# A two-block transformer forward pass: one queue for the first inputs, norm factors applied later, wider MLP entries, and the RWKV chunk matrices kept as 64x64 blocks

## The chip, the cores and the metric

The kernel runs on one core of a Trainium2 chip. The metric is the device time of one execution in microseconds; the time before is the median of three runs. A profiled execution, taken by the hardware profiler, gives the trace. TensorE is called PE here, its weight load PEld, VectorE DVE, ScalarE ACT, GpSimd POOL and SyncE SP.

## The reference

The input x has 256 tokens of 1024 features, in float32. Two blocks follow one another. The part that the change rewrites most is the RWKV7 recurrence of the first block:

```python
def rwkv7_scan(r, w, k, v, a_vec, b_vec):
    """S_t = S_{t-1} diag(w_t) + (S_{t-1} a_t) b_t^T + v_t k_t^T ; y_t = S_t r_t. All (B,T,H,N)."""
    def step(s, inp):
        r_t, w_t, k_t, v_t, a_t, b_t = inp
        sa = jnp.einsum('bhvk,bhk->bhv', s, a_t)
        s = s * w_t[:, :, None, :] + sa[..., None] * b_t[:, :, None, :] + v_t[..., None] * k_t[:, :, None, :]
        return s, jnp.einsum('bhvk,bhk->bhv', s, r_t)

def first_block(x, ...):
    h = rms_norm(x, mix_norm_g)
    x = x + hybrid_mixer(h, ...)   # h @ w_in; short conv, stick-breaking attention, RWKV7, spatial gating,
                                   # four sigmoid gates over their projections, @ w_o
    h = rms_norm(x, ffn_norm_g)
    x = x + conv_glu_ffn(h, w_up, ffn_conv_w, w_down)
    return rms_norm(x, final_norm_g)

def second_block(x, mem, ...):     # layer 0: pool mixer, layer 1: sliding-window attention with sinks
    for l in range(2):
        proj = rmsnorm(h, norm_mix[l]) @ w_in[l]
        main, mq = proj[..., :768], proj[..., 768:]
        main_out = pool_mixer(main, ...) if l == 0 else swa_sink_attention(...)
        mem_out = memory_attention(...)
        h = h + jnp.concatenate([main_out, mem_out], axis=-1) @ w_out[l]
        h = h + sq_relu_mlp(rmsnorm(h, norm_mlp[l]), w_up[l], w_down[l])
    return h
```

The recurrence has 4 heads of 64 channels. The pool mixer takes, in 4 groups of 192 channels, the mean over the last 2, 4, 8 or 16 tokens less the token itself, and multiplies each group by a 192x192 matrix.

## The kernel before

**Products.** Every weight is loaded from HBM by `load_split` (L193): SP issues the transfer to a buffer `raw`, ACT casts it to fp32r (`wh`), DVE subtracts (`wl` = raw − wh). There are four buffers of each. A product is then three fp32r matmuls into one PSUM group (`mm3`, L207): high by high, high by low, low by high. I call these the main matmuls. The small products of the mixers are plain fp32, and in the trace an fp32 product is two instructions.

**Order.** PE's order is the order in which the program issues its products. The main line of the program issues groups of main matmuls and calls `tick()` (L234) after each. `tick()` lets every generator that was put `beside` the main line go on by its rate (0.5 steps a tick unless given, 0.6 for RWKV, L897); a generator issues one step of small work and yields. `finish()` runs generators to their end at once. The work within `urgent()` gets a higher priority on DVE and ACT.

**The start.** Seven cold matmuls on a zeroed buffer run while the inputs come. ACT issues the five transfers of xT (L464), SP those of the weights; `split_scaled` makes the pair `xp` of x times the norm's gain, and `fm_part` multiplies it by blocks 9 and 7 of `w_in`, piece by piece of xT (`z_first`). The norm's factor per token is not applied to x but later to the products: a generator (`input_norm`) sums the squares, POOL raises the mean to the power −0.5 (`rtok`, L379), and PE spreads it over the partitions. For the RWKV columns this is used in `shifted`, which `finish()` (after block 6) precedes.

**RWKV.** `rwkv()` (L556) works on 4 chunks of 64 tokens, two chunks to a half `b` of 128 tokens. For each half and head it makes the products of `bt` and `ktl` with `ar` (64 channels deep), masks them to the two chunks on the diagonal (`at`, 128x128 for each head), inverts the triangular matrix by doubling in five levels (`LEVELS`), and then goes over the chunks one by one: `rc`, `uc`, the state `st`, and the output `yt`. In the inversion X, Y and PX are 128x128 for each head with zeros off the two 64x64 blocks. A level makes one product X,at, one Y,PX and (but for the last) a transposition of Y, for four heads and both halves. The masked products, in the words of the code:

```python
at = [mt([P, 2, 4, P], "at", bufs=4) for _ in range(2)]
...
def level(b, lhs, rhs, w):
    o = psum("A")
    for h in range(4):
        TE.matmul(o[:, 64 * h : 64 * h + 64], lhs[:, h], half(rhs[:, h], w), start=True, stop=True)
    return packed(o)
```

**MLP entry.** Each MLP multiplies by `w_up` in blocks of 256 features (`fm_blocks`, L271), each by halves of the 1024 input features. The first 512 input features are ready before the others: after the first half of the first block's product, `finish(first_half)` issues the transpositions and pairs (`features`) that make the rest.

**Pool layer.** `main_block` makes the main columns by blocks, `pool_tile` the windowed means of 128 channels (a product with `bands`, then `dd` on DVE and the pair `dp`), `pool_product` the 192x192 products of a group, which end in the pair `y`. `out_half` multiplies four of the eight blocks of `y` by `w_out2` and adds the sum; it runs twice, first for blocks 4 to 7 and after `pool_product(0)` for 0 to 3. Memory attention (`att`, two generators) runs beside.

## Time and profile before

| | |
|---|---|
| median of 3 runs | 1030.14 us (1028.31 to 1031.03) |
| profiled execution, its own time | 1030.78 us |
| its span | 1028.9 us, 16258 instructions |
| PE busy | 1009.8 us (98% of the span), 6216 matmul instructions |
| DVE busy | 699.2 us (68%) |
| ACT busy | 558.2 us (54%) |
| POOL busy | 142.7 us (14%) |
| DMA | 176.39 MB, mean 171 GB/s |

The span goes from the first instruction to the last; 1.9 us of the profiled execution lie around it. Busy is the share of the span in which an engine has an instruction under way. A PE row gives the time from the first start to the last end of a run of equal instructions, and matmuls are pipelined, so that what a matmul costs is the distance from its start to the next one's, and not its length. A wait in square brackets is the idle time of the engine just before the row, with what ended it.

### The profile page before, as it was taken

How to read it: one execution, taken by the hardware profiler on the slowest of the kernel's cores; microseconds unless marked ns; L12 is line 12 of the kernel's file. 1: busy time of each engine (PE TensorE's matmuls, PEld its weight loads, DVE VectorE, ACT ScalarE, POOL GpSimd, SP SyncE). 2: the span in 40 equal slices, each digit the busy share in tenths (PEclk: the TensorE clock that was granted, in tenths of full speed). 3: DMA queues.
4: the chain of work that ended last, by engine and by line, in shares of the span. 5: the costliest groups of instructions: out<-in, count | busy, mean ns of one | idle time of the engine just before them, and what ended most of it. 6: DMA issues, size and time to landing. Idle time of an engine off the chain costs nothing.

```text
span 1028.9 us, 16258 instructions
## 1 busy us (share of the span) xinstructions
PE 1009.8 (98%) x6216; PEld 876.8 (85%) x6216; DVE 699.2 (68%) x1101; ACT 558.2 (54%) x966; POOL 142.7 (14%) x137
## 2 busy tenths in 40 slices
PE   8999999999999999999999999999999999999998
PEld 7889987778899999988888888888898668888886
DVE  4787467687747888865576777746467877776452
ACT  5653556454557655545664655535365556555432
POOL 0110001121000000001210244400011103443000
PEclk9999999999999999999999999999999999999999
DMA  8535353356555555565534455555553325555661
GB/s 288 181 122 162 111 179 110 127 176 243 174 184 205 190 184 183 184 189 186 179 120 154 161 195 188 184 189 187 199 210 122 103 90 172 185 188 186 191 217 63
DMA packets 50590, 176.39 MB, mean 171 GB/s; under 512 B 5776, under 2 KB 6928, under 8 KB 50128
## 3 DMA queue, kind: packets, MB, share of 16 engines
q1 hardware_dynamic: 49392, 173.51, 51.0%
q10 hardware_dynamic: 1008, 1.57, 0.4%
q8 instruction: 49, 0.80, 0.3%
q0 software_dynamic: 112, 0.27, 0.1%
q14 instruction: 29, 0.24, 0.1%
HBM read 174.28 MB, written 1.05 MB: 170 GB/s over the span
## 4 chain that ended last, share of the span: by engine, by line
PE 88%; DVE 7%; ACT 2%; issue 1%; POOL 1%; DMA 1%; ACTq 0%; DVEq 0%; POOLq 0%
PE mm L126 76%; PE ps L126 11%; DVE wl L203 3%; ACT wh L202 1%; DMA a<-in_xT 0%; DMA raw<-in_w_in 0%; DVE a L343 0%; POOL a L1131 0%; DVE a L349 0%; DVE sc L346 0%; DVE mxs L1175 0%; ACT sc L1193 0%; DVE yt L349 0%; DVE sq L349 0%; POOL r L379 0%
## 5 line engine op out<-in xcount | busy, mean ns | idle before, releaser
L203 DVE TENSOR_TENSOR wl<-raw,wh 128x1024 fp32r<-128x1024 f32 (+2 forms) x318 | 387.3, 1219 | 237.9 <-ACT wh L202 236.0
L202 ACT CAST wh<-raw 128x1024 fp32r<-128x1024 f32 (+2 forms) x318 | 328.4, 1034 | 348.9 <-PE mm L126 315.9
L126 PE MATMUL mm<-a,wh 128*128 128x256 f32 (+1 forms) x1536 | 370.1, 323 | 2.9 <-DVE a L343 2.2
L126 PE MATMUL mm<-a,wl 128*128 128x256 f32 x1024 | 288.5, 282 | 0.0
L126 PEld LDWEIGHTS mm<-a,wh 128*128 128x128 f32 x1536 | 256.2, 190 | 30.3 <-DVE a L343 4.3
L126 PEld LDWEIGHTS mm<-a,wl 128*128 128x128 f32 x1024 | 194.8, 190 | 0.2 <-issue 0.2
L126 PE MATMUL mm<-wh,u 128*128 128x512 f32 x512 | 158.6, 389 | 0.0
L126 PE MATMUL mm<-wh,a 128*128 128x512 f32 (+1 forms) x512 | 145.8, 358 | 0.0
L126 PEld LDWEIGHTS mm<-wh,u 128*128 128x128 f32 x512 | 96.1, 188 | 20.0
L1249 POOL TENSOR_TENSOR u<-gate,u 128x256 fp32r<-128x256 f32 x64 | 84.5, 1322 | 170.2 <-ACT u L1248 119.8
L126 PEld LDWEIGHTS mm<-wh,a 128*128 128x128 f32 x512 | 91.0, 189 | 14.1 <-issue 1.2
L126 PE MATMUL mm<-wl,u 128*128 128x512 f32 x256 | 99.6, 389 | 0.0
L126 PE MATMUL mm<-wl,a 128*128 128x512 f32 (+1 forms) x256 | 90.0, 352 | 0.0
L126 PEld LDWEIGHTS mm<-wl,u 128*128 128x128 f32 x256 | 48.1, 188 | 9.8
L126 PE MATMUL mm<-wh,ff 128*128 128x512 f32 x176 | 54.9, 390 | 0.0
L126 PEld LDWEIGHTS mm<-wl,a 128*128 128x128 f32 x256 | 48.5, 190 | 5.5
L126 PE MATMUL mm<-wh,y 128*128 128x512 f32 x128 | 43.2, 406 | 0.9 <-ACT y L338 0.5
L346 DVE SCALAR_TENSOR_TENSOR cv<-mm,pv,cv 128x255 f32<-128x255 f32 x88 | 42.2, 479 | 1.7 <-ACT cv L1093 0.2
L126 PEld LDWEIGHTS mm<-wh,ff 128*128 128x128 f32 x176 | 33.0, 188 | 6.9
L126 PE MATMUL mm<-wl,ff 128*128 128x512 f32 x88 | 34.3, 389 | 0.0
L346 DVE SCALAR_TENSOR_TENSOR gate<-gate 128x256 f32<-128x256 f32 x64 | 31.9, 501 | 2.0
L349 DVE TENSOR_TENSOR gate<-mm,gate 128x256 f32<-128x256 f32 (+1 forms) x68 | 29.5, 434 | 3.7 <-ACT gate L1245 2.9
(342 smaller groups left out, 1188.1 us busy)
## 6 DMA issues: line engine op xcount, KB each, us to landing
raw<-in_w_up SPq DMA_DIRECT2D x108, 512.0 KB, 4.4
raw<-in_w_dn SPq DMA_DIRECT2D x86, 512.0 KB, 4.3
raw<-in_w_in SPq DMA_DIRECT2D x36, 512.0 KB, 3.8
raw<-in_w_gate SPq DMA_DIRECT2D x32, 512.0 KB, 3.7
raw<-in_w_out SPq DMA_DIRECT2D x16, 512.0 KB, 3.8
raw<-in_outs SPq DMA_DIRECT2D x8, 512.0 KB, 3.6
raw<-in_w_mkv SPq DMA_DIRECT2D x8, 512.0 KB, 3.6
raw<-in_w_o SPq DMA_DIRECT2D x8, 512.0 KB, 4.4
```

The source lines that it names most:

```text
L126: ins = f(*a, **k)
L202: S.copy(wh[:, :m], raw[:, :m])
L203: V.tensor_tensor(out=wl[:, :m], in0=raw[:, :m], in1=wh[:, :m].bitcast(F32), op=ALU.subtract)
L346: return V.scalar_tensor_tensor(out=o, in0=a, scalar=sc, in1=b, op0=op0, op1=op1)
L349: return V.tensor_tensor(out=o, in0=a, in1=b, op=op)
L1249: G.tensor_tensor(out=u.l[:, n], in0=sq, in1=u.h[:, n].bitcast(F32), op=ALU.subtract)
```

## The change

- xT's transfers are issued by SP, each piece ahead of the weights that it is multiplied with; the constants `cm`, `ci` and `cb`, which SP issued between the weights, come later.
- Blocks 6 and 8 of `w_in` are both multiplied before `finish()`; then the factor is applied to all four blocks.
- The RWKV matrices are kept as two blocks of 64x64, one below the other (`[P, 4, 64]` in place of `[P, 4, 128]`). `chunks` multiplies each chunk's block on its own 64 rows and its own 64 columns of the array: rows 0 to 63 with columns 0 to 63 of the output, rows 64 to 127 with 64 to 127, into one PSUM buffer. The transposition of Y is a product with a 64x64 identity. The products with `ar` are issued by chunk and by head of a pair, the two heads of a pair into different buffers. `rc` and `uc` are no longer zeroed.
- Two more yields stand ahead of the transposition of `yt`, the rate of `rwkv` is 0.65, memory attention has one yield more, `features` is urgent.
- `fm_blocks` begins with the first halves of two blocks (four PSUM buffers) ahead of `finish(first_half)`.
- In the pool layer `out_half` is no longer used there: `pool_product(0)` comes directly behind the last `pool_tile`, and each half of the output columns is one product over all eight blocks of `y`, in the order 4, 2, 0, 6, with `finish(*atts)` ahead of 6.

The diff, cut to its core:

```diff
@@ -285,11 +285,19 @@
-        for i, src in enumerate(srcs):
+        os_ = [psum_mm(), psum_mm(), psum_mm(), psum("M")]
+        for a in (0, 4):
+            if a:
+                finish(first_half)
+            for i in range(2):
+                w = load_split(srcs[i][:, a : a + 4], 4)
+                for j in range(2):
+                    part(os_[2 * i + j], w, j, a, a + 4)
+                    if a:
+                        yield os_[2 * i + j]
+        for src in srcs[2:]:
...
             for a in (0, 4):
-                if a and not i:
-                    finish(first_half)
@@ -330,8 +338,9 @@
                 TE.transpose(o[:, i * P : i * P + P], h[:, j, k * P : k * P + P], ident)
-            for k in (k0, k0 + 1):
-                use(k, o[:, (k - k0) * T : (k - k0) * T + T])
+            with urgent():
+                for k in (k0, k0 + 1):
+                    use(k, o[:, (k - k0) * T : (k - k0) * T + T])
@@ -458,11 +467,6 @@
-    FIRST = ((0, 1), (1, 2), (2, 4), (4, 6), (6, 8))
-    xT = t8()
-    for a, b in FIRST:
-        nc.scalar.dma_start(out=xT[:, a:b], in_=I["xT"][:, a:b])
@@ -490,15 +494,16 @@
-    xp = pair8()
+    xT, xp = t8(), pair8()
     z_first = {b: psum("M") for b in (3, 1)}
-    for a, b in FIRST:
+    for a, b in ((0, 1), (1, 2), (2, 4), (4, 6), (6, 8)):
+        nc.sync.dma_start(out=xT[:, a:b], in_=I["xT"][:, a:b])
...
     CB = load_const(cp, "cb")
-    ident, bones, ones = CB("ident"), CB("bones"), CB("ones")
+    ident, bones, ones, ident2 = CB("ident"), CB("bones"), CB("ones"), CB("ident2")
@@ -533,17 +538,14 @@
-    for b in (0, 2):
-        o = fm_block(I["w_in"][6 + b], xp)
-        if b == 0:
-            finish()
-            for z in (3, 1):
-                shifted(z, z_first[z])
-            wlo = q2("wlo", "A")
-            nc.sync.dma_start(out=wlo, in_=I["lora"])
-            CM = load_const(m1, "cm")
-            CI = load_const(m1, "ci")
+    z_first.update((b, fm_block(I["w_in"][6 + b], xp)) for b in (0, 2))
+    finish()
+    for b, o in z_first.items():
         shifted(b, o)
+    wlo = q2("wlo", "A")
+    nc.sync.dma_start(out=wlo, in_=I["lora"])
+    CM = load_const(m1, "cm")
+    CI = load_const(m1, "ci")
@@ -628,24 +630,40 @@
+        chunk = [slice(0, CH), slice(CH, P)]
+        def chunks(o, n, lhs, rhs):
+            for h in range(4):
+                for c in chunk:
+                    TE.matmul(o[c, n * h : n * h + n], lhs(h, c), rhs(h, c), start=True, stop=True)
+            return o[:, : 4 * n]
...
         for b in range(2):
-            bs = slice(b * P, b * P + P)
-            at = [mt([P, 2, 4, P], "at", bufs=4) for _ in range(2)]
-            for h in range(4):
-                j, hs = h // 2, slice(64 * (h % 2), 64 * (h % 2) + 64)
-                o = psum("A")
+            at = [mt([P, 2, 4, CH], "at", bufs=4) for _ in range(2)]
+            o = [psum("A") for _ in range(2)]
+            for j in range(2):
                 for i, src in enumerate((bt, ktl)):
-                    TE.matmul(o[:, 256 * i : 256 * i + 256], src[hs, j, bs], ar[hs, :, j, bs], start=True, stop=True)
-                o4 = o.rearrange("p (i a t) -> p i a t", i=2, a=2)
+                    for c in chunk:
+                        tk = slice(b * P + c.start, b * P + c.stop)
+                        for e in range(2):
+                            at_ = (2 * j + i) * P
+                            TE.matmul(o[e][c, at_ : at_ + P], src[chunk[e], j, tk], ar[chunk[e], :, j, tk],
+                                      start=True, stop=True)
+            for e in range(2):
+                o4 = o[e].rearrange("p (j i a t) -> p a i j t", j=2, i=2, a=2)
                 for a in range(2):
-                    tt(at[a][:, :, h], o4[:, :, a], over(CM("mar")[:, a * P : a * P + P], 2))
+                    tt(at[a][:, :, e::2], o4[:, a], CM("mar")[:, a * CH : a * CH + CH].rearrange(
+                        "p (i j t) -> p i j t", i=1, j=1).to_broadcast([P, 2, 2, CH]))
...
-            X, Y, PX = (q2(n, "A", shape=(P, 4, P)) for n in ("X", "Y", "PX"))
+            X, Y, PX = (q2(n, "A", shape=(P, 4, CH)) for n in ("X", "Y", "PX"))
             G.memset(PX, 0.0)
-            S.copy(X, over(ident, 4))
-            S.copy(Y, over(ident, 4))
+            S.copy(X, over(ident2, 4))
+            S.copy(Y, over(ident2, 4))
@@ -653,13 +671,11 @@
         for b in range(2):
-            o = psum("A")
-            for h in range(4):
-                TE.transpose(o[:, h * P : h * P + P], atA[b][:, 0, h], ident)
+            o = chunks(psum("A"), CH, lambda h, c: atA[b][c, 0, h], lambda h, c: ident2[c])
...
         for m in LEVELS:
-            nb = P // (2 * m)
+            nb = CH // (2 * m)
@@ -668,30 +684,24 @@
             def packed(o):
-                return o[:, :256].rearrange("p (h n m) -> p h n m", h=4, m=m)
+                return o.rearrange("p (h n m) -> p h n m", h=4, m=m)
...
-            def level(b, lhs, rhs, w):
-                o = psum("A")
-                for h in range(4):
-                    TE.matmul(o[:, 64 * h : 64 * h + 64], lhs[:, h], half(rhs[:, h], w), start=True, stop=True)
-                return packed(o)
+            def level(lhs, rhs, w):
+                return packed(chunks(psum("A"), CH // 2, lambda h, c: lhs[c, h], lambda h, c: half(rhs[c, h], w)))
...
             for b in range(2):
-                S.copy(half4(Pm[b], 0), level(b, atA[b][:, 0], Xm[b], 0))
+                S.copy(half4(Pm[b], 0), level(atA[b][:, 0], Xm[b], 0))
...
             for b in range(2):
-                V.copy_predicated(half4(Ym[b], 1), lmask(f"my{m}"), level(b, Pm[b], Ym[b], 1))
+                V.copy_predicated(half4(Ym[b], 1), lmask(f"my{m}"), level(Pm[b], Ym[b], 1))
...
                 for b in range(2):
-                    o = psum("A")
-                    for h in range(4):
-                        TE.transpose(o[:, h * P : h * P + P], Ym[b][:, h], ident)
-                    S.copy(flat(Xm[b]), o)
+                    S.copy(flat(Xm[b]), chunks(psum("A"), CH, lambda h, c: Ym[b][c, h], lambda h, c: ident2[c]))
@@ -708,23 +718,22 @@
             rc, uc = scr([P, 256], "rc", "A"), scr([P, 256], "uc", "A")
-            G.memset(rc, 0.0)
-            G.memset(uc, 0.0)
...
             o = psum("A")
-            for h in range(4):
-                vs = slice(64 * h, 64 * h + 64)
-                TE.matmul(o[cs, vs], atA[b][:, 1, h, cs], vtk[:, b, vs], start=True, stop=(c == 0))
-                if c:
-                    TE.matmul(o[cs, vs], ar[:, 0, h // 2, tk], st[:, h], start=False, stop=True)
+            vss = [slice(64 * h, 64 * h + 64) for h in range(4)]
+            last = lambda h: h == 3
+            for h, vs in enumerate(vss):
+                TE.matmul(o[cs, vs], atA[b][cs, 1, h], vtk[cs, b, vs], start=(h == 0), stop=(c == 0 and last(h)))
+            if c:
+                for h, vs in enumerate(vss):
+                    TE.matmul(o[cs, vs], ar[:, 0, h // 2, tk], st[:, h], start=False, stop=last(h))
...
             o = psum("A")
-            for h in range(4):
-                vs = slice(64 * h, 64 * h + 64)
-                TE.matmul(o[cs, vs], Ym[b][:, h, cs], rc[:, vs], start=True, stop=True)
+            for h, vs in enumerate(vss):
+                TE.matmul(o[cs, vs], Ym[b][cs, h], rc[cs, vs], start=True, stop=True)
@@ -749,12 +758,13 @@
             o = psum("A")
-            for h in range(4):
-                vs = slice(64 * h, 64 * h + 64)
-                TE.matmul(o[cs, vs], atR[b][:, 1, h, cs], vtk[:, b, vs], start=True, stop=False)
-                if c:
-                    TE.matmul(o[cs, vs], ar[:, 1, h // 2, tk], st[:, h], start=False, stop=False)
-                TE.matmul(o[cs, vs], atR[b][:, 0, h, cs], uc[:, vs], start=False, stop=True)
+            for h, vs in enumerate(vss):
+                TE.matmul(o[cs, vs], atR[b][cs, 1, h], vtk[cs, b, vs], start=(h == 0), stop=False)
+            for h, vs in enumerate(vss):
+                TE.matmul(o[cs, vs], atR[b][cs, 0, h], uc[cs, vs], start=False, stop=(c == 0 and last(h)))
+            if c:
+                for h, vs in enumerate(vss):
+                    TE.matmul(o[cs, vs], ar[:, 1, h // 2, tk], st[:, h], start=False, stop=last(h))
@@ -790,6 +800,8 @@
         tt(yt, yt, sq, ALU.add)
+        yield
+        yield
@@ -894,7 +906,7 @@
-    rw = beside(rwkv(), 0, 0.6)
+    rw = beside(rwkv(), 0, 0.65)
@@ -1204,6 +1216,8 @@
                 ts(sc[:, a, at(tb)], sc[:, a, at(tb)], rc[:, i : i + 1])
+        if swa is None:
+            yield
@@ -1358,19 +1372,32 @@
-    beside(tiles((5, 4, 3, 2)))
+    tl = beside(tiles((5, 4, 3, 2)))
...
     main_block(0)
+    finish(tl)
...
     pool_tile(0)
-    finish()
     h1 = tok8()
-    out_half(0, 4, y, residual, h1)
...
     g, sums, done = to_mlp(0)
-    tf = out_half(0, 0, y, lambda j, c: h1[:, j, c], h1, done)
+    for cb in range(2):
+        o = [psum_mm() for _ in range(2)]
+        for a in (4, 2, 0, 6):
+            if a == 6:
+                finish(*atts)
+            w = load_split(I["w_out2"][0, cb, :, a : a + 2], 2, 512)
+            for j in range(2):
+                for k in (a, a + 1):
+                    mm3(o[j], y[:, k, j * P : j * P + P], w[:, k - a], k == 4, k == 7)
+                tick()
+        c = slice(512 * cb, 512 * cb + 512)
+        for j in range(2):
+            with urgent():
+                tt(h1[:, j, c], o[j], residual(j, c), ALU.add)
+        tf = done(h1, cb)
```

How the order moves, on SP and PE.

SP's queue at the start, before (`raw` is a weight, `a` here is xT, `cb`, `cm`, `ci` are constants):

```order
L459 DMA pv<-in_pv 128x248
L200 DMA raw_99<-in_w_in 128x256
L200 DMA raw_111<-in_w_in 128x256
L200 DMA raw_125<-in_w_in 128x256
L200 DMA raw_137<-in_w_in 128x256
L447 DMA cb_269<-in_cb 128x384
```

and after:

```order
L468 DMA pv<-in_pv 128x248
L500 DMA a_3_88<-in_xT 128x256
L201 DMA raw_95<-in_w_in 128x256
L201 DMA raw_107<-in_w_in 128x256
L500 DMA a_3_88<-in_xT 128x256
L201 DMA raw_122<-in_w_in 128x256
```

The first piece of xT now stands second in SP's queue and the second piece fifth, where ACT issued them before.

PE in one level of the inversion, before: a transposition of Y for both halves between main matmuls.

```order
L126 MATMUL mm_1078<-a_4_94,wl_1123 128x256
L126 MATMUL ps_1139<-cb_269,Y_875 128x128 x4
L126 MATMUL ps_1145<-cb_269,Y_933 128x128 x4
L126 MATMUL mm_1078<-a_4_94,wh_1122 128x256 x2
L126 MATMUL mm_1078<-a_4_94,wl_1123 128x256
```

and after, the same place:

```order
L127 MATMUL mm_1118<-a_4_89,wl_1121 128x256
L127 MATMUL ps_1137<-cb_269,Y_865 64x64 x8
L127 MATMUL ps_1147<-cb_269,Y_907 64x64 x8
L127 MATMUL mm_1118<-a_4_89,wh_1120 128x256 x2
L127 MATMUL mm_1118<-a_4_89,wl_1121 128x256
```

Four transpositions of 128x128 have become eight products of 64x64; the steps X,at and Y,PX change in the same way, from 128x64 x4 to 64x32 x8.

PE at the end of the pool layer, before (`bands` belongs to the last `pool_tile`, `y` to the product with `w_out2`, `dp` to `pool_product(0)`):

```order
L126 MATMUL mm_5745<-bands,uh 128x256
L126 MATMUL mm_5745<-bands,ul 128x256
L126 MATMUL mm_5755<-wh_5758,y_5239 128x512
L126 MATMUL mm_5755<-wl_5759,y_5239 128x512
L126 MATMUL mm_5755<-wh_5758,y_5239 128x512 x2
```

and after:

```order
L127 MATMUL mm_5847<-bands,uh 128x256
L127 MATMUL mm_5847<-bands,ul 128x256
L127 MATMUL mm_5863<-dp_5358,wh_5858 128x256
L127 MATMUL mm_5872<-dp_5358,wh_5858 128x256
L127 MATMUL mm_5884<-dp_5358,wh_5858 128x256
L127 MATMUL mm_5884<-dp_5359,wh_5858 128x256
```

Behind the last bands 48 matmuls with `y` stood before the first with `dp`; now the first with `dp` stands there.

## Rows read from the trace of the kernel before

**Rows 1.** the page: the chain that ended last, share of the span by engine

```profile
PE 88%; DVE 7%; ACT 2%; issue 1%; POOL 1%; DMA 1%; ACTq 0%; DVEq 0%; POOLq 0%
```

**Rows 2.** PE's waits by releaser: us in total, times, longest us

```profile
PE ps L126 <- ACT a L342: 3.0, 1, 3.0
PE ps L126 <- POOL rtok L379: 2.2, 1, 2.2
PE mm L126 <- DVE a L343: 2.2, 4, 1.1
PE ps L126 <- DVE yt L349: 2.1, 1, 2.1
...
PE ps L126 <- DVE sc L353: 0.8, 2, 0.7
PE ps L126 <- DVE uc L728: 0.7, 1, 0.7
...
PE mm L126 <- DVE y L343: 0.3, 1, 0.3
```

**Rows 3.** windows: length, busy us (x) of PE, PEld, DVE, ACT, POOL; PEclk, DMA

```profile
10.40:14.30 3.90, 3.82 (x17) 3.60 (x18) 2.52 (x7) 2.66 (x7) 0.00 (x0) 0.56 1.03 388
14.30:20.00 5.70, 5.70 (x50) 5.70 (x49) 4.69 (x9) 3.70 (x8) 0.00 (x0) 1.00 0.76 247
66.00:78.00 12.00, 11.24 (x71) 8.68 (x70) 11.23 (x27) 6.71 (x9) 0.53 (x1) 1.00 0.26 89
```

**Rows 4.** timeline of the start: start, us, engine, instruction, [idle before]

```profile
0.74 5.21 ACTq L464 DMA_DIRECT2D a<-in_xT  x5
...
1.19 6.33 PE L126 MATMUL mm<-cold 128*128 128x256 f32 x14 [1.19 <-DVE cold L476]
...
10.48 1.10 PE L126 MATMUL ps<-a,wh 128*128 128x256 f32 x3 [2.95 <-ACT a L342]
...
23.79 0.40 PE L126 MATMUL mm<-a,wh 128*128 128x256 f32 x2
```

**Rows 5.** timeline of PE around a step X,at and around sgw,vg

```profile
84.55 1.90 PE L126 MATMUL ps<-X,at 128*128 128x64 f32 x16
...
86.26 0.48 PE L126 MATMUL mm<-a,wh 128*128 128x256 f32 x2
...
86.94 0.28 PE L126 MATMUL mm<-a,wl 128*128 128x256 f32 x1
...
87.14 0.66 PE L126 MATMUL ps<-sgw,vg 128*64 128x128 f32 x8
...
87.73 0.50 PE L126 MATMUL mm<-a,wh 128*128 128x256 f32 x2
```

**Rows 6.** groups by form: names, shapes, xcount | busy us, mean ns

```profile
L126 PE MATMUL ps<-cb,Y 128*128 128x128 f32 x32 | 4.1, 272 | 0.0
```

**Rows 7.** timeline of PE in a state update

```profile
154.90 0.22 PE L126 MATMUL ps<-vtk,ktm 64*64 64x64 f32 x1
154.90 0.27 PE L126 MATMUL ps<-uc,btm 64*64 64x64 f32 x2
154.96 0.22 PE L126 MATMUL ps<-vtk,ktm 64*64 64x64 f32 x1
```

**Rows 8.** windows, ar alone, sum of 3 stretches

```profile
sum 6.59, PE 6.22 PEld 4.11 DVE 0.00; mean PE 2.07 PEld 1.37 DVE 0.00
```

**Rows 9.** timeline of PE, products with ar

```profile
69.04 0.38 PE L126 MATMUL ps<-ar,ktl 64*128 64x256 f32 x1
69.25 0.38 PE L126 MATMUL ps<-ar,bt 64*128 64x256 f32 x1
69.25 0.38 PE L126 MATMUL ps<-ar,ktl 64*128 64x256 f32 x1
```

**Rows 10.** timeline at the end of the pool layer

```profile
541.39 0.28 PE L126 MATMUL mm<-bands,ul 128*128 128x256 f32 x1
...
542.82 0.86 ACT L338 CAST dp<-dd 128x256 fp32r<-128x256 f32 x2 [2.15 <-DVE dd L349]
```

19 lines of the change are left out of this document (9 added, 10 removed).

## The prediction

> **What bounds the kernel now.** I read the page first: the chain of work that ended last lies 88% on PE [rows 1]. So the time is the sum of PE's instructions and of the few places where PE waits, and an edit counts only if it shortens one of the two. PE's own waits, grouped by releaser, are the second view: there is one long wait for each of ACT a (3.0), POOL rtok (2.2) and DVE yt (2.1), and a few shorter ones [rows 2]; those shown are 11.3 us of a span of 1028.9. Third come the windows of the start: after its first idle stretch PE gets a granted clock of 0.56 from 10.4 to 14.3 and does 17 matmuls there, where the next 5.7 us hold 50 at clock 1.00 [rows 3]. Last, the timelines, for what a small product costs and what it costs to go to it and come back.
>
> The sum is made against the profiled execution, 1030.78 us. The median of the runs shown is 0.64 lower, within their spread, so I don't correct for it. I take 0.3%, about 3.1 us, as the least difference that a measurement of this kernel can tell from none.
>
> **1. The start.** ACT issues the five xT transfers for 5.21 us and only then loads its tables, and the first real matmul stands at 10.48, after 2.95 us of idle; the cold matmuls, which begin at 1.19, are done at 7.52 (1.19 + 6.33) [rows 4]. The phase of 96 matmuls of 120 ns (17 in 3.90 us at the low clock, 50 in 5.70 at the full one [rows 3]) would be 11.5 us long; it takes 13.3, from 10.48 to the next phase at 23.79 [rows 4]. After, SP issues the first piece of xT directly after pv, ahead of the weights, and ACT has no issues and one table load fewer in front of its first casts. If the first casts end before 7.5, PE goes on without a gap: 10.48 − 7.5 = 3.0, and 13.3 − 11.5 = 1.8 if the clock then stays at 1.00, since PE was busy and granted 1.00 up to there. Five more issues stand ahead of the later weights on SP's queue, and cb, cm and ci, which stood ahead, go behind; I take off 0.5 for one late piece. Bounds: 0 (the low clock stays and the data are no earlier) and −5.3 (no late piece, and the last cold matmul followed at once). **−4.3.**
>
> **2. Norm factors.** rtok's spread over the partitions stands 4 real matmuls behind its sum before and 12 after, so 8 more of 120 ns cover the wait of 2.2 [rows 2]: **−1.0**, between 0 and −2.2.
>
> **3. RWKV matrices.** One product of the levels is now eight 64x64 tiles on the diagonal (rows and columns 0–63, then 64–127) in place of four full ones. In the trace an fp32 product is two instructions. Before: one step X,at is 16 instructions from 84.55 to 86.26, 1.71 us or 107 ns each, and leaves one following matmul 0.1 late [rows 5]. Ten steps (80 instructions X,at, as many Y,PX) make 17.1. The transposes cb,Y are 32 instructions in four trips, 4.1 us busy [rows 6]; a fifth trip (cb,at) makes 5.1, and some 0.2 of each lies over the next matmul: 4.1. Together 21.2. After: 160 + 160 + 128 + 32 = 480 instructions. What a 64x64 product costs shows in the state updates: their starts come two at a time, 0.06 us from pair to pair [rows 7], so 29 ns each: 13.9. These pairs share the rows and differ in columns; pairs on the diagonal of the array are not in the trace, and that is this sum's open point (rivals). Going to a narrow tile and back costs more than to a full one: before sgw,vg the last matmul takes 0.20 (86.94 to 87.14) in place of 0.12, the eight products take 0.59 where four pairs at X,at's 0.11 would be 0.44, and the two matmuls behind take 0.50 [rows 5] where two take 0.40 [rows 4], some 0.35 in all; two matmuls behind X,at take 0.48, a trip of 0.09. So 0.26 for each of 15 trips (10 steps, 4 + 1 transposes): +3.9. Sum: 13.9 + 3.9 − 21.2 = **−3.4**. That the evictions on ACT and DVE are half as wide helps, since DVE is busy 11.23 of 12.0 us from 66 to 78 [rows 3], but PE is fed by main matmuls there, so I count nothing.
>
> The products with ar: 32 instructions in three stretches, 6.59 us [rows 8]. After, 64 of half the columns, in four quadrants. Where bt and ktl run in pairs, a pair follows the one before it by 0.21 [rows 9]. After, in pairs and at half the columns, 32 × 0.105 = 3.4; and there are half the evictions to wait for, 0.3. 6.6 + 0.3 − 3.4 = **−3.5**, between −2.5 (waits stay) and −5 (four at once).
>
> The chunk steps keep their number of products, but change tile shape three times more: **+0.4**. Three main matmuls now stand between rc's product and the state's in every chunk; the wait for uc, 0.7 in one chunk [rows 2], can come up in the others: **+0.5**, between −0.7 and +1.8.
>
> **4. yt.** Two steps more before the transposes, at a higher rate. As many main matmuls as before (36) stand between the bonus product and the transposes, but on DVE one foreign operation lies between the bonus's copy and yt's last addition where four lay. If the three are 0.7 long on average, the wait of 2.1 [rows 2] goes, with 0.1 of restart: **−2.2**, at least −1.
>
> **5. Entries of the two MLPs.** Their first halves are now 32 matmuls in front of finish(first_half), 5.6 us, where 16 (2.8 us) stood. The wait for DVE a (2.2 in four places, 1.1 the longest [rows 2]) ends; with the restarts of the weight load that the waits view leaves out, 2.6: **−2.6**, at least −1.5. What comes next is the same work of ACT and DVE with twice the cover.
>
> **6. Pool layer.** A further step in memory attention takes away the wait for sc, 0.8 [rows 2]. In return the product of group 0 now stands right behind the last bands, where 48 matmuls with y stood. Its input is not ready: the last band starts at 541.39, and the cast to dp, behind dd on DVE, ends at 543.68 (542.82 + 0.86) [rows 10]. PE, ready at 541.51, waits some 2.1. The wait for DVE y ahead of the last w_out2 products, 0.3 [rows 2], goes, with its restart 0.5. −0.8 + 2.1 − 0.5 = **+0.8**, at most +2.5. The four DVE additions that are gone lie beside PE, at nothing; where features are now urgent the order of DVE and ACT is that of before, at nothing too.
>
> **Sum:** −4.3 − 1.0 − 3.4 − 3.5 + 0.4 + 0.5 − 2.2 − 2.6 + 0.8 = −15.3, so 1030.8 − 15.3 = 1015.5, taken as **1015**. With the bounds above, its own range is 1008 to 1022.
>
> **Rivals.** *The diagonal pairs take turns.* Both tiles of a pair write the same PSUM bank, in other partitions. In the trace products on different rows (bt and ktl with ar, both at 69.25 [rows 9]) run in pairs, but write different banks; the pairs that share a bank [rows 7] differ in columns alone. Neither is the new case. If they take turns, the 480 products cost 58 ns each: 27.8 + 3.9 − 21.2 = +10.5 in place of −3.4, and the kernel takes 1015.5 + 13.9 = **1029**. For it: all pairs on different rows avoid a common bank in this code. Against: a tile pair on the diagonal shares neither rows, columns nor partitions, and both nearest rows show pairs. The Trainium skill, TensorEngine Tiling (Array Packing), section Restrictions and Gotchas, says that different row tiles cannot access the same PSUM bank at one time, which speaks against this edit: by it the pairs take turns. No row of this trace shows it either way.
>
> *The weight load isn't covered (slower).* If a small product cannot load its weights while the one before it still runs in another tile, it costs what X,at costs, 107 ns [rows 5], for a quarter of the work: 480 × 0.107 + 3.9 − 21.2 = +34, with the −11.9 of the rest +22, **1053**. It decides from 61 ns on (480 × 0.061 + 3.9 − 21.2 = 12.0, the gain of all the rest), and shows as slower from 67. Against it: the state updates, at 29 ns each [rows 7], can't have an uncovered load.
>
> *New waits.* The tighter distances (products behind the bands, steps at a rate of 0.65, uc in three chunks) together cost 6 more than counted, or the start gains nothing: **1020**. For it: DVE is near full from 66 to 78 [rows 3]. Against: away from the places counted PE has hardly waited at the old distances, and most have grown.
>
> **How the numbers follow.** Forecast 0.70; turns 0.18; new waits 0.07; load not covered 0.05. The predicted time is the forecast's, 1015. The range reaches from its low end, 1008, to the rival of the turns, 1029, and leaves out the slower rival and some of both tails. Faster by over 0.3% is below 1027.1: forecast, new waits and a small part of the turns, 0.79; within 0.3%, 0.15 (turns, beside better luck elsewhere); slower 0.06.
>
> **What would show it.** In the changed trace the first real matmul should stand near 7.5 with granted clock 1.00 up to 20; the wait for ACT a in the start should be gone. Sixteen instructions of a level's step should take some 0.5 us for one half of the sequence, the 480 together some 14 to 18; about 28 us says turns, 50 the uncovered load. The waits for yt and for DVE a in front of the MLPs should be gone, rtok's about 1.2, and a new one of about 2 should stand behind the last bands, for ACT or DVE dp. The ar products should take about 3.4 us. The forecast is wrong if PE's start-to-start time of a 64x64 product on the diagonal is 50 ns or more, or if waits of PE above 1 us stand in new places.

## The result, and the profile after

| | before | changed |
|---|---|---|
| median | 1029.22 us (1026.40 to 1031.03, 4 runs) | 1016.11 us (1015.11 to 1016.87, 4 runs) |
| profiled execution | 1030.78 us, span 1028.9 | 1015.11 us, span 1013.3 |
| ratio | | 0.9874, 95% interval 0.9848 to 0.9901 |

The kernel is some 13 us faster; 1015 was forecast. In the experiment with full-size matrices one of eight executions took 1223.95 us at a granted clock of 0.75; the time given there is the median of the other seven. The page of the changed kernel, busy times and the chain that ended last:

```profile
PE 999.4 (99%) x6528; PEld 866.8 (86%) x6528; DVE 690.0 (68%) x1089; ACT 553.9 (55%) x965; POOL 143.4 (14%) x129
...
PE 89%; DVE 5%; DMA 2%; ACT 2%; issue 1%; POOL 1%; SPq 0%; DVEq 0%; ACTq 0%; POOLq 0%
```

PE is 10.4 us less busy, though it executes 312 instructions more (6528 for 6216), and the chain lies on PE as it did [rows 1]. The rest of the 15.6 us between the two spans is waits.

PE's waits by releaser, in the same columns as [rows 2]:

```profile
PE mm L127 <- ACT dp L347: 1.4, 1, 1.4
PE ps L127 <- ACT wh L203: 1.3, 1, 1.3
...
PE mm L127 <- DVE ul L355: 0.9, 1, 0.9
PE ps L127 <- POOL rtok L388: 0.8, 1, 0.8
PE mm L127 <- DVE dp L348: 0.7, 2, 0.4
PE mm L127 <- DVE gate L355: 0.7, 1, 0.7
PE ps L127 <- DVE ktl L358: 0.6, 1, 0.6
...
PE mm L127 <- DVE a L358: 0.2, 1, 0.2
...
PE mm L127 <- DVE a L352: 0.2, 1, 0.2
```

The waits for ACT a (3.0), DVE yt (2.1), DVE sc (0.8) and DVE uc (0.7) of [rows 2] are gone, those for DVE a have shrunk from 2.2 to 0.2 and 0.2, rtok's from 2.2 to 0.8. New are ACT wh (1.3, at the start), ACT dp (1.4) and DVE dp (0.7), both at the end of the pool layer, and DVE gate (0.7, ahead of `wh,ysg` at 189.10, beside RWKV); DVE ul and ktl have grown.

Where the time went shows best in the starts of the same product in the two traces. The products of the main line stand in the same order at these places:

| start of the first product | before | changed | change of the stretch up to it | forecast |
|---|---|---|---|---|
| behind the first phase (`mm<-a,wh`) | 23.79 | 20.99 | −2.8 | −4.3 |
| LoRA products (`th,wlo`) | 43.09 | 39.30 | −1.0 | −1.0 |
| `wh,yrw`, behind all of RWKV | 244.19 | 230.80 | −9.6 | −8.2 |
| `cb,qsq`, layer 0 | 517.27 | 503.53 | −0.35 | 0 |
| first MLP's `w_up`, behind the pool layer | 568.23 | 556.12 | +1.6 | +0.8 |
| first MLP's `w_dn` | 661.03 | 647.44 | −1.5 | −2.6 for both MLPs |
| second MLP's `w_up` | 844.25 | 830.32 | −0.3 | 0 |
| second MLP's `w_dn` | 937.73 | 922.18 | −1.6 | (in the −2.6) |
| last matmul | 1024.56 | 1009.02 | 0 | 0 |

Minus is shorter. The sum is −15.5, and −15.3 was forecast. Two stretches were mis-sized by over a microsecond, against each other: the start gained less, RWKV more.

The start, in windows as in [rows 3]:

```profile
7.00:9.00 2.00, 1.95 (x17) 1.74 (x15) 0.90 (x3) 0.91 (x2) 0.00 (x0) 1.00 0.73 196
9.00:11.00 2.00, 0.50 (x2) 0.30 (x2) 0.93 (x2) 0.85 (x2) 0.00 (x0) 1.00 0.92 328
11.00:13.00 2.00, 1.99 (x10) 1.99 (x11) 1.59 (x4) 2.00 (x5) 0.00 (x0) 0.58 0.87 326
13.00:15.00 2.00, 2.00 (x13) 2.00 (x11) 1.89 (x4) 1.62 (x4) 0.00 (x0) 0.57 0.80 220
```

From 9 to 11 PE does two matmuls: it has run out of weights. From 11 to 15 it has, for most of the time, the low clock again (0.50 would be 1.2 GHz throughout, 1.00 is 2.4), as before from 10.4 to 14.3 [rows 3].

One step X,at of the levels for both halves, on PE's timeline (compare [rows 5], where 16 instructions take 1.71 us):

```profile
74.10 0.28 PE L127 MATMUL mm<-a,wl 128*128 128x256 f32 x1
74.31 1.12 PE L127 MATMUL ps<-X,at 64*64 64x32 f32 x32
75.36 0.50 PE L127 MATMUL mm<-a,wh 128*128 128x256 f32 x2
```

and the groups by form (busy, mean ns; compare [rows 6]):

```profile
L127 PE MATMUL ps<-X,at 64*64 64x32 f32 x160 | 5.6, 220 | 0.0
...
L127 PE MATMUL ps<-cb,Y 64*64 64x64 f32 x128 | 4.6, 221 | 0.0
...
L127 PE MATMUL ps<-cb,at 64*64 64x64 f32 x32 | 1.1, 221 | 0.0
```

The 32 instructions take 1.05 us with the change back to the full tile, and their starts come two at a time, 0.006 apart, 0.058 from pair to pair. 29 ns each is what the forecast took from the state updates [rows 7]. The matmul ahead takes 0.21, the two behind 0.50, as around sgw,vg [rows 5]. By the starts the way to the narrow tiles and back costs 0.31 here: 0.21 + 1.05 + 0.22, from the matmul ahead to the second one behind, where 0.12 + 0.93 + 0.12 would do without it.

The products with ar in the second half:

```profile
66.07 0.45 PE L127 MATMUL ps<-ar,bt 64*64 64x128 f32 x8
66.34 0.40 PE L127 MATMUL ps<-ar,ktl 64*64 64x128 f32 x8
66.56 0.40 PE L127 MATMUL ps<-ar,bt 64*64 64x128 f32 x8
66.78 0.40 PE L127 MATMUL ps<-ar,ktl 64*64 64x128 f32 x8
67.11 0.39 PE L127 MATMUL mm<-wh,a 128*128 128x256 f32 x1
```

Groups of eight follow one another by 0.22 (66.34 to 66.56 to 66.78). Eight of 128 columns in that time are four at once, where [rows 9] show two of 256 columns in 0.21. The whole of ar takes 0.38 (60.92 to 61.30), 0.81 (62.32 to 63.13) and 1.04 (66.07 to 67.11), 2.2 us for 6.59 [rows 8].

The end of the pool layer, to be read against [rows 10]:

```profile
525.26 0.28 PE L127 MATMUL mm<-bands,ul 128*128 128x256 f32 x1
526.07 0.86 ACT L347 CAST dp<-dd 128x256 fp32r<-128x256 f32 x2 [0.97 <-DVE dd L358]
...
526.98 0.62 PE L127 MATMUL mm<-dp,wh 128*128 128x256 f32 x3 [1.44 <-ACT dp L347]
...
528.01 0.38 PE L127 MATMUL mm<-dp,wh 128*128 128x256 f32 x1 [0.41 <-DVE dp L348]
```

The last band starts at 525.26, the first product with dp at 526.98, and the fourth waits again for dp's low part: the new wait of 1.44 and 0.41. With the restarts it is 2.27: 2.75 from the last band to the fourth product, where four steps of 0.12 would do.

### The profile page after: what moved, and what is told of

Read it like the earlier page. It is cut to its first block, busy times and chain, and to the rows that moved or that the text cites. A ratio compares the mean times of both kernels' runs of the same rounds, so it can differ in the third digit from the quotient of the medians.

```text
span 1013.3 us, 16847 instructions
## 1 busy us (share of the span) xinstructions
PE 999.4 (99%) x6528; PEld 866.8 (86%) x6528; DVE 690.0 (68%) x1089; ACT 553.9 (55%) x965; POOL 143.4 (14%) x129
## 3 DMA queue, kind: packets, MB, share of 16 engines
HBM read 174.10 MB, written 1.05 MB: 173 GB/s over the span
## 4 chain that ended last, share of the span: by engine, by line
PE 89%; DVE 5%; DMA 2%; ACT 2%; issue 1%; POOL 1%; SPq 0%; DVEq 0%; ACTq 0%; POOLq 0%
PE mm L127 79%; PE ps L127 11%; DVE wl L204 2%; DMA raw<-in_w_in 1%; DMA wlo<-in_lora 1%; ACT wh L203 1%; ACT sc L1205 0%; POOL a L1143 0%; DVE sc L355 0%; DVE mxs L1187 0%; DVE a L352 0%; DVE dd L358 0%; DVE ssa L358 0%; DVE dp L348 0%; ACT ssq L373 0%
## 5 line engine op out<-in xcount | busy, mean ns | idle before, releaser
L127 PE MATMUL mm<-a,wh 128*128 128x256 f32 (+1 forms) x1520 | 364.2, 322 | 1.0 <-ACT a L351 0.6
L127 PE MATMUL mm<-a,wl 128*128 128x256 f32 x1008 | 284.0, 282 | 0.0
L127 PEld LDWEIGHTS mm<-a,wh 128*128 128x128 f32 x1520 | 253.1, 190 | 26.5 <-ACT a L351 1.2
L127 PEld LDWEIGHTS mm<-a,wl 128*128 128x128 f32 x1008 | 191.8, 190 | 0.1
L1143 POOL TENSOR_TENSOR a<-a,gfb 128x512 f32<-128x512 f32 x4 | 7.1, 1790 | 177.1 <-issue 149.8
```

The source lines that it names most:

```text
L127: ins = f(*a, **k)
L1143: G.tensor_tensor(out=y3[:, j, c], in0=x3[:, j, c], in1=gfb[:, c], op=ALU.mult)
```

## The experiments

Each kernel is the changed one with the edit shown. Differences in microseconds that are smaller than the medians can tell are taken from the starts of the products in the table above. Each time one stretch is compared, so that a shift in an earlier one does not count.

### Full-size matrices

```diff
-            X, Y, PX = (q2(n, "A", shape=(P, 4, CH)) for n in ("X", "Y", "PX"))
+            X, Y, PX = (q2(n, "A", shape=(P, 4, P)) for n in ("X", "Y", "PX"))
...
-                return packed(chunks(psum("A"), CH // 2, lambda h, c: lhs[c, h], lambda h, c: half(rhs[c, h], w)))
+                for h in range(4):
+                    TE.matmul(o[:, 64 * h : 64 * h + 64], lhs[:, h], half(rhs[:, h], w), start=True, stop=True)
```

> The changed kernel with the RWKV matrices and the ar products back at full size (128x128 on all rows and columns), all else as changed. Theory (small tiles run in pairs, four at a time for ar): the stretch from the LoRA products to rw_out loses the matrices' gain (3 to 5 us) and that of the ar products (3.5 to 4), so +7 to +8 over the changed kernel, about 1023. Rival (the stretch got shorter through the tighter steps and the order around yt, not through the tiles): less than +4, below 1020.

Measured 1023.26 us, ratio 0.9933 (0.9910 to 0.9956). The stretch from the LoRA products to `wh,yrw` is 7.3 longer (+0.4 at its start, +7.7 at its end), and all stretches behind it are equal within 0.4. The tiles carry this gain, not the order of the steps; 6.5 was forecast for them (3.4 + 3.5 − 0.4). The wider evictions on ACT and DVE come back with this edit as well; the next run leaves them narrow and changes the order alone.

### The halves in turn

```diff
-            for h in range(4):
-                for c in chunk:
+            for c in chunk:
+                for h in range(4):
                     TE.matmul(o[c, n * h : n * h + n], lhs(h, c), rhs(h, c), start=True, stop=True)
```

> The changed kernel, but each product of the 64x64 matrices issues its four heads of the first half and then its four of the second, so that neighbours in the queue use the same rows and columns. Theory (29 ns is a pair's 58 divided by two): 480 x 0.029 = +14 over the changed kernel, about 1030, with starts 58 ns apart inside a half. Rival (29 ns is what a small product costs by itself): no change, 1016.

Measured 1021.32 us, ratio 0.9928 (0.9908 to 0.9948). The stretch of RWKV is 5.1 longer (+0.6 to +5.7): neither 0 nor 14. The groups by form:

```profile
L127 PE MATMUL ps<-X,at 64*64 64x32 f32 x160 | 7.1, 222 | 0.0
...
L127 PE MATMUL ps<-cb,Y 64*64 64x64 f32 x128 | 6.2, 224 | 0.0
...
L127 PE MATMUL ps<-cb,at 64*64 64x64 f32 x32 | 1.5, 224 | 0.0
```

X,at and Y,PX grow from 5.6 to 7.1 each, cb,Y from 4.6 to 6.2, cb,at from 1.1 to 1.5: 5.0. Inside a half the starts are 58 ns apart, as the theory says; but the halves do not follow one another. In the first step X,at, counted from its first start, eight instructions start at 0, 0.08, 0.14, 0.20, 0.25, 0.31, 0.37 and 0.43 us, and eight more at 0.26, 0.34, 0.40, 0.46, 0.51, 0.57, 0.63 and 0.69. The trace does not name an instruction's tile; but the first eight in the queue share one tile, so the start at 0.26, 6 ns behind the fifth, must be the second half's first. PE thus pairs instructions on different tiles that are not neighbours in the queue, which the forecast of 14 had not allowed for. That pairs are what makes 29 ns holds: in one tile alone such an instruction costs 58. The order alone costs 5.1, more than what the levels have of the 7.3 above (some 2.9, an estimate: 7.3 less the 4.4 that the ar products gained). So narrow tiles that pair only in part are in sum slower here than full ones.

### A longer cold start

```diff
-    for _ in range(7):
+    for _ in range(11):
         TE.matmul(o, cold[:, :P], cold, start=True, stop=True)
```

> The changed kernel with 11 cold matmuls in place of 7, so that the first real matmul starts some 1.7 us later, near 7.5, and PE should not run out of weights at 8.7. Theory (the low clock at 11.0 to 14.7 follows PE's idle stretch): no idle, granted clock 1.00 throughout, the first phase ends at about 19.0 in place of 20.99, -2.0 us, about 1014. Rival (the clock falls in that stretch whatever PE did before): clock 0.50 there again, the phase ends at 20.7 or later, between -0.3 and +1.7.

Measured 1016.37 us, ratio 0.9885 (0.9863 to 0.9907): no gain. Windows (us, busy, counts, PEclk):

```profile
10.00:16.00 6.00, 5.78 (x48) 5.56 (x47) 4.34 (x9) 4.65 (x10) 0.00 (x0) 1.00 0.86 266
29.00:31.00 2.00, 0.44 (x4) 0.23 (x2) 1.60 (x3) 0.24 (x1) 1.38 (x1) 1.00 0.65 217
31.00:33.00 2.00, 1.78 (x11) 1.78 (x12) 0.63 (x2) 0.37 (x1) 0.42 (x2) 0.72 0.76 244
33.00:35.00 2.00, 2.00 (x11) 2.00 (x11) 1.25 (x3) 0.77 (x1) 0.00 (x0) 0.50 0.88 277
35.00:37.00 2.00, 2.00 (x18) 2.00 (x17) 1.69 (x3) 2.00 (x6) 0.00 (x0) 0.92 0.96 373
```

As the theory said, PE has no idle stretch at 9 and keeps clock 1.00 from 10 to 16. But the first phase ends at 20.53, not 19.0, and the LoRA products start at 43.03, 3.7 later than in the changed kernel. (0.8 of that is order: seven main matmuls more stand ahead of them in this kernel's queue, though the edit doesn't touch them. At `wh,yrw` 2.3 are left.) At the end of the first phase PE waits 0.6 for wh, then 0.8 for wl and 1.8 for rtok, and behind that idle stretch comes the low clock that was absent before, 0.50 from 33 to 35. The rival on the clock falls, and with it the thought that the low clock was what kept the start from its gain. The profiled execution took 1018.72; 1.3 of it is another low clock, behind the bands (last section).

### The old order in the pool layer

```diff
...
-    finish(tl)
     pool_product(1)
     tick()
     pool_tile(1)
     pool_tile(0)
+    finish()
     h1 = tok8()
+    out_half(0, 4, y, residual, h1)
     pool_product(0)
     g, sums, done = to_mlp(0)
-    for cb in range(2):
...
+    tf = out_half(0, 0, y, lambda j, c: h1[:, j, c], h1, done)
```

> The changed kernel with the end of the pool layer as it was: finish, the product of blocks 4 to 7 of y, then pool_product(0), then blocks 0 to 3; memory attention's further step stays. Theory (the changed order costs PE a wait behind the last bands that 48 matmuls covered): -1.6 for the zone's measured loss and -0.8 for the step that stays, -2.4 in all, about 1014, with no wait for dp behind the bands. Rival (the zone's loss comes from memory attention's new step, or the single product saves as much elsewhere): 0 or slower.

Measured 1011.80 us, ratio 0.9844 (0.9819 to 0.9868). From `cb,qsq` to the MLP it takes 49.46 where the changed kernel takes 52.59: −3.1, and 50.96 before. Behind the last band no wait is left:

```profile
524.60 0.28 PE L127 MATMUL mm<-bands,ul 128*128 128x256 f32 x1
524.72 0.39 PE L127 MATMUL mm<-wh,y 128*128 128x512 f32 x1
```

So this part of the change costs 3.1 us, more than my +2.1 − 0.5: the wait for DVE ul in the third product of pool_product(1) (0.94, a buffer that comes free late) goes too. The further step in memory attention, which stays here, brings its gain. One wait comes up with the old order: 0.97 for DVE a behind the first halves of the first MLP (561.89), whose stretch is 0.2 longer.

### xT issued by ACT

```diff
-        nc.sync.dma_start(out=xT[:, a:b], in_=I["xT"][:, a:b])
+        nc.scalar.dma_start(out=xT[:, a:b], in_=I["xT"][:, a:b])
```

(ahead of the loop, as before.)

> The changed kernel with xT's five transfers issued by ACT again and the constants ahead of the later weights; all else as changed. Theory (ACT's issues delay its first casts, PE idles some 3 us and gets the low clock behind that): first real matmul near 10.5, clock 0.50 to 0.56 for some 4 us, first phase ended near 23.8; the changed kernel's four profiles so far end it between 19.6 and 21.0, so +2.8 to +4.2, about 1019.5. Rival (the first data come no earlier by the one queue): less than +1.

Measured 1018.94 us, ratio 0.9890 (0.9863 to 0.9916).

```profile
1.19 6.04 PE L127 MATMUL mm<-cold 128*128 128x256 f32 x14 [1.19 <-DVE cold L485]
10.97 1.10 PE L127 MATMUL ps<-a,wh 128*128 128x256 f32 x3 [3.75 <-ACT a L351]
```

The first real matmul stands at 10.97 after 3.75 of idle, and the first phase ends at 25.30, 4.3 later. But the LoRA products start at 42.22, only 2.9 later: rtok's wait, 0.8 in the changed kernel, isn't there, nor are waits for weights. What the earlier start gains, these take back in part. Against before (43.09) the same number gives 0.9 for the later norm factors and the rest of what changed at the start; both numbers come from single profiles, and the start of the LoRA products spreads by 1.7 among profiles of one start (table below).

### The narrow entry, and features without urgency

```diff
-        os_ = [psum_mm(), psum_mm(), psum_mm(), psum("M")]
-        for a in (0, 4):
...
+        for i, src in enumerate(srcs):
+            o = [psum_mm() for _ in range(2)]
+            for a in (0, 4):
+                if a and not i:
+                    finish(first_half)
```

> The changed kernel with fm_blocks as before: the first half of one block, 16 matmuls, ahead of finish(first_half). Theory: the waits for DVE a of 0.9 to 1.1 come back behind the first half in both MLPs, +1.3 to +1.9 for each, +3 in all, about 1019. Rival (features being urgent has taken those waits away by itself): 0 to +0.5.

```diff
-            with urgent():
-                for k in (k0, k0 + 1):
-                    use(k, o[:, (k - k0) * T : (k - k0) * T + T])
+            for k in (k0, k0 + 1):
+                use(k, o[:, (k - k0) * T : (k - k0) * T + T])
```

> The changed kernel with features without urgent. Theory (urgency took about half of the wait ahead of the MLPs' second halves, as the run with the narrow entry suggests): with the wide entry's twofold cover in place the waits stay away, so 0 to +0.4 in each MLP. Rival (the wide entry does little by itself): +0.7 in each, with waits for DVE a behind the first halves.

With the narrow entry 1017.11 us, ratio 0.9878 (0.9848 to 0.9909); PE's wait:

```profile
PE mm L127 <- DVE a L344: 0.9, 3, 0.4
```

Without urgency 1016.27 us, ratio 0.9848 (0.9824 to 0.9872):

```profile
PE mm L127 <- DVE a L351: 0.4, 2, 0.2
```

By stages from `w_up` to `w_dn`: before 92.8 and 93.5, changed 91.3 and 91.9, narrow 92.1 and 91.1, not urgent 91.3 and 91.9. The theory on the narrow entry, +3 in all, fails: 0.39 of waiting comes back in each MLP, for 0.74 and 1.10 before, and the two stages together are as long as in the changed kernel (183.2). So the wide entry alone takes the waits away, and urgency alone takes more than half of them (0.9 is left of 2.2). The medians, 1.0 and 0.2 above that of the changed kernel, say no more than this; both profiles also have a low clock behind the bands, outside these stages. The narrow form's second MLP is even 0.8 shorter than the wide one's, in spite of 0.4 us more of waiting; its 512-column matmuls follow one another by 0.230 us where they do so by 0.235 in the changed kernel (medians of the starts in that stage). I found no cause for that.

### The old steps of RWKV

```diff
-    rw = beside(rwkv(), 0, 0.65)
+    rw = beside(rwkv(), 0, 0.6)
...
         tt(yt, yt, sq, ALU.add)
-        yield
-        yield
         yield
```

> The changed kernel with rwkv at a rate of 0.6 and without the two further yields ahead of the transposition of yt. Theory (the distance to yt was what was missing): the wait for yt is back at some 2 us, +2.2, about 1018. Rival (DVE reaches yt earlier since its RWKV operations are half as wide): a wait under 0.7, and no more than +0.7.

Measured 1019.51 us, ratio 0.9898 (0.9869 to 0.9926). The stretch of RWKV is 2.9 longer (+0.7 at its start, +3.6 at its end), and two waits are there:

```profile
PE ps L127 <- DVE yt L358: 2.1, 1, 2.1
...
PE ps L127 <- DVE uc L737: 1.3, 1, 1.3
```

The theory on yt holds, for the rate and the yields together; neither was undone alone. A wait for uc comes back with it, longer than the 0.7 before, and none is left in the changed kernel, where I had counted it at +0.5. The new wait for DVE gate (0.7) isn't there with the old steps: it is a price of the new ones.

### Five raw buffers

```diff
-        raw = wp.tile([P, size], F32, name=nm("raw"), tag=tag + "raw", bufs=bufs)
+        raw = wp.tile([P, size], F32, name=nm("raw"), tag=tag + "raw", bufs=bufs + 1)
```

> The changed kernel with five raw buffers for weights in place of four. Theory (at the start SP's queue stands still until DVE frees a raw buffer, and xT's next piece stands behind): the stall of 0.9 to 1.5 near 9 us shrinks by half or more, the waits for wh and wl at 19 to 21 that three profiles show go, the first phase ends below 19.3; -1, about 1015. Rival (the transfers themselves are the limit): the second stall or the first stays at its length, the phase ends between 19.6 and 21.0.

Measured 1013.99 us, ratio 0.9841 (0.9816 to 0.9867). The waits for wl and wh behind the first phase are gone, the one at 10 stays at 1.0, the phase ends at 20.48, and the LoRA products start at 40.01, behind waits of 0.5 for the squares' sum and 0.8 for rtok. That is the rival's picture. The median is some 2 us below those of the changed kernel, but its trace shows no stretch that would give as much: `wh,yrw` starts at 230.20, where the two profiles of the changed kernel have 230.80 and 230.47, and all behind it is equal. I count it as nothing.

### The changed kernel again

> The changed kernel itself, on the same chip as the next three. The start varied in the profiles of kernels with the same start (first phase ended at 19.6 to 21.0), and three of eight showed a fall of the clock behind the wait at the bands. So 1014 to 1017, with or without a low clock of some 1.5 us length behind the wait at the bands.

Measured 1015.79 us, ratio 0.9845 (0.9822 to 0.9867). Span 1013.1, and every start behind RWKV within 0.35 of the first profile; the start again with a wait for ACT wh (1.5) and the low clock behind it, and none behind the bands.

### Memory attention's step behind the bands

```diff
     pool_product(1)
-    tick()
     pool_tile(1)
     pool_tile(0)
+    tick()
```

> The changed kernel with the tick that issues memory attention's eight transpositions (1.03 us) moved from ahead of the last two pool tiles to behind them; the rest of the new order stays. Theory (PE only lacks work behind the bands): the bands and the chain behind them start 1.0 earlier and the transpositions fill 1.0 of the wait, -0.9 to -1.1 and a wait for dp of 0.4 to 0.7. Rival (the chain is held by DVE and ACT, which do other work first): the wait stays over 1, less than -0.5.

Measured 1014.78 us, ratio 0.9832 (0.9809 to 0.9855). The stretch from `cb,qsq` to the MLP is 51.69 for 52.59: −0.9.

```profile
525.34 0.42 DVE L358 TENSOR_TENSOR dd<-mm,inv 64x256 f32<-64x256 f32 x1 [0.19 <-PE mm L127]
...
525.55 1.04 PE L127 MATMUL ps<-cb,sc 128*128 128x128 f32 x8
525.70 0.48 DVE L352 SCALAR_TENSOR_TENSOR y<-mm,pv,y 128x256 fp32r<-128x256 f32 x1
526.20 0.88 DVE L358 TENSOR_TENSOR dd<-mm,inv 64x256 f32<-64x256 f32 x2
...
526.97 0.58 ACT L1232 COPY pT<-ps 128x512 f32<-128x512 f32 x1
...
527.90 0.73 PE L127 MATMUL mm<-dp,wh 128*128 128x256 f32 x4 [1.31 <-ACT dp L347]
```

The gain is the theory's, the wait the rival's: 1.31 of it is left, since DVE, which now meets the bands earlier, does a product's y (0.48 at 525.70) between the pieces of dd, and ACT copies what the transpositions made (0.58 at 526.97) between its two casts to dp. The second wait, for dp's low part ahead of the fourth product, is what went. Covering such a wait by PE's work alone is not enough; the chain behind it has to be free as well.

### All together

The old order in the pool layer, five raw buffers, and one more step ahead of rtok's spread:

```diff
         power(rtok, mean_sq(sqs, "B"))
         yield
+        yield
         spread_sb(rtok, rs, "B")
```

> The changed kernel with the end of the pool layer as it was, one more step of the main products ahead of rtok's spread (24 matmuls in place of 12) and five raw buffers. Theory: -3.1 for the pool layer (the run with that order undone), -1.0 for rtok's wait, and 0 to -0.5 from the raw buffers, -4 to -4.6 against the changed kernel in the same call, about 1011. Rival (the low clock and the waits for weights move elsewhere): -3 or less.

Measured 1009.99 us, ratio 0.9795 (0.9772 to 0.9818), where the changed kernel, run again beside it, has 1015.79 and 0.9845 (0.9822 to 0.9867): −5.8 by the medians, −5.3 by the last matmul's start. PE's largest waits but for the first:

```profile
PE mm L127 <- DVE a L352: 1.1, 2, 1.0
PE ps L127 <- ACT wh L203: 1.0, 1, 1.0
PE mm L127 <- DVE gate L355: 0.7, 1, 0.7
```

No wait for rtok or ul, none for dp but 0.3 ahead of pool_product(1), and no low clock in the start or behind the bands. The stretch up to `wh,yrw` is 2.3 shorter than in the second profile of the changed kernel, where 1.0 to 1.5 was expected, and the pool layer 3.1. The step ahead of rtok was not run by itself, so the 2.3 can't be split. This is the fastest version.

## Why the prediction was right, step by step

**What bounds the kernel** held: PE's instructions and its waits make up the whole difference. That the sum came within 0.2 of the measured −15.5 is in part luck: the start gained 1.5 less than its term, RWKV 1.4 more. And by one of the signs that I set, a wait of PE above 1 us in a new place, the forecast failed at the start: 1.3 for ACT wh. (The wait of 1.4 behind the bands was foretold.)

**1. The start: right direction, term too large.** 2.8 in the first profile, and 3.4 in the mean of the nine below, for 4.3. Two numbers in the term were wrong. I let the first real matmul follow cold matmuls that end at 7.5, as before, and took them to run at a granted clock of 1.00; they ran at the low clock up to its rise (last section), which came earlier here, and the first matmul stood at 5.74. And "0.5 for one late piece" is the term that failed: the phase of 11.5 us loses 3.8 in the first profile, 1.5 of it by 15 matmuls at 0.213 in place of 0.12 us under the low clock that was to be away, the rest by waits for wh and wl. The nine profiles of kernels with this start:

| kernel | clock rises | wait for ACT wh near 9 us | PEclk, 10 to 16 | first phase ends | LoRA products |
|---|---|---|---|---|---|
| changed | 4.48 | 1.3 | 0.72 | 20.99 | 39.30 |
| changed again | 4.78 | 1.5 | 0.72 | 21.26 | 38.93 |
| step behind the bands | 4.68 | 1.3 | 0.72 | 21.17 | 40.25 |
| narrow entry | 5.82 | 1.1 | 1.00 | 19.94 | 38.92 |
| full matrices | 5.93 | 1.0 | 1.00 | 20.61 | 39.70 |
| old pool order | 5.26 | 0.9 | 1.00 | 19.60 | 38.60 |
| halves in turn | 5.64 | 0.7 | 1.00 | 19.79 | 39.91 |
| not urgent | 6.26 | 0.4 | 1.00 | 19.75 | 39.64 |
| old steps | 7.25 | none over 0.2 | 1.00 | 20.60 | 40.04 |

A wait of 0.4 to 1.5 stands near 9 in all but one. It ends between 10.20 and 10.72 in all eight, when the next weights are cast; what differs is how soon PE gets there, and the three that get there first, since their clock rose first, have the low clock behind the wait. Yet at the LoRA products the three stand at 39.5 in the mean, and so do the other six: whoever gets through the first phase sooner waits behind it, for weights, for rtok, or for wlo, the weights of the LoRA products. This last wait is new (0.3 to 1.0 in six of the nine): the change issues the transfer of wlo 7.7 us ahead of its use (31.65 to 39.30), where it was 10.4 before (32.65 to 43.09). The start is held by what arrives and by the norm's chain, not by PE. The term should have been taken from that, and read at 43 us and not at 24: −2.9, by the run with ACT's queue.

**2. Norm factors: the wait fell as foretold, the −1.0 is not shown by itself.** It is −1.0 in the table and 0.9 by the run with ACT's queue, but in the mean of the nine profiles the stretch from the first phase to the LoRA products is only 0.2 shorter than before (19.1 for 19.3). The two terms of the start trade with each other from run to run; together they came to −3.6 in that mean, for −5.3. rtok's wait fell to 0.8, and to none in two of the nine, where 1.2 was expected.

**3. RWKV: mechanism right, one size off.** The pairs on the diagonal run at 29 ns, and a trip costs 0.31, for the 0.35 read around sgw,vg. The rival of the turns falls: both tiles of a pair write one PSUM bank at starts 6 ns apart. The Trainium skill, TensorEngine Tiling (Array Packing), section Restrictions and Gotchas, has it that different row tiles cannot access the same bank at one time; this trace does not agree, with 29 ns each for pairs on different rows, different columns and one bank. The rival of the uncovered load falls by the same 29 ns. The ar products ran four at once, 2.2 us for the 3.4 that I took: −4.4, between my −3.5 and the bound of −5. ktl's wait grew from 0.3 to 0.6 and a wait of 0.7 for DVE gate came up; they took some back. The chunk steps were to cost +0.9; the uc wait is gone instead. Sum −9.6 for −8.2 with yt.

**4. yt: right.** The wait is gone, and comes back at 2.1 with the old steps.

**5. MLP entries: right sum, incomplete reason.** −3.1 for −2.6. I put the urgency of features at nothing since the orders of DVE and ACT at the layer's end looked alike; the run with the narrow entry shows that urgency alone would have taken more than half of those waits. By the two stages (186.3 before, 183.2 changed, 183.2 narrow, 183.3 not urgent) either edit would have done nearly all of it, the narrow one with the unexplained 0.8.

**6. Pool layer: the wait as foretold, two more not.** 1.44 + 0.41 and their restarts, 2.27, for the 2.1 expected. Beside it came 0.57 ahead of pool_product(1) (the low part of the last tile's dp) and 0.4 more at DVE ul. +1.6 for +0.8. This was the one part of the change that loses time, and undoing it is worth 3.1.

## What to carry to other kernels

Small products on tiles that share neither rows nor columns are worth interleaving: pairs on the diagonal cost half, and quadrants a quarter, of the same products in one tile; the trip into and out of the narrow tiles (0.31 us here) has to be earned by each group. A gain at the start should be read where the stages join again, not where it arises, and from more than one profile. A clock of 1.00 in a window may mean that none was recorded there; the distance of equal matmuls tells. An engine that is the bound should not be put directly behind a chain of other engines: the order that took 48 matmuls from behind the bands costs 3.1 us, as much as the wider cover at both MLP entries gained.

## What was not expected of the hardware

**The low clock behind waits varies from run to run.** The same wait of 1.4 us behind the bands stands in ten profiles; in four of them (halves in turn, longer cold, narrow entry, not urgent) the granted clock falls behind it, in six it doesn't. It costs 1.3 to 1.4 us each time, by the stretch to the MLP. In the run with the halves in turn:

```profile
530.00:535.00 5.00, 3.15 (x23) 2.75 (x22) 3.93 (x8) 1.64 (x4) 0.00 (x0) 0.97 0.55 159
535.00:540.00 5.00, 5.00 (x25) 3.83 (x23) 2.62 (x4) 2.31 (x4) 0.00 (x0) 0.69 0.22 87
```

In the changed kernel the same stretches have PEclk 1.00 throughout. So a wait that is taken away is worth more, on average, than its length.

**The clock rises at a different time in each run, and the windows don't show it.** Before, eight cold matmuls from 3.91 on:

```profile
3.91 3.61 PE L126 MATMUL mm<-cold 128*128 128x256 f32 x8
```

and in the changed kernel the same eight:

```profile
3.91 2.17 PE L127 MATMUL mm<-cold 128*128 128x256 f32 x8
```

The windows give a clock of 1.00 for both. But the trace's own list of granted clocks begins only at 7.38 us before and at 4.48 in the changed kernel, each time with 1.00, and the windows count a stretch that no entry covers as 1.00 too. The starts say what it was: the cold matmuls are 0.427 us apart before, to the last one, and in the changed kernel 0.427 up to the start at 4.34 and 0.215 from 4.63 on. All fourteen traces agree: 0.427 up to the list's first entry and, where cold matmuls are left, half of it behind. So the cold matmuls run at the low level (1.2 GHz) until the clock rises. The rise comes anywhere between 4.48 and 7.25 us in the nine kernels with one start, though PE has been at the same cold matmuls from 1.19 on in all of them, and the first real matmul follows the last cold one by 0.03 to 0.07 us: that is why it could come at 5.74. With xT on ACT's queue the rise came at 6.79. What sets its moment is open.

**PE pairs instructions that are not neighbours in its queue**, as the starts in the run with the halves in turn show: the ninth instruction of a step beside the fifth.
